# A decoder trunk on one core: moving the first weight part and the first root in the lead, and scaling the last rows on two engines

## The chip, the cores and the metric

The kernel runs on one core of a Trainium2 chip. The metric is the device time of one execution in microseconds (us). The engines work side by side, each with its own queue of instructions: PE (TensorE, matrix products and transposes), DVE (VectorE), ACT (ScalarE), POOL (GpSimd), and SP (SyncE), which here only issues transfers. Transfers are carried out by the core's 16 DMA engines; SP, ACT and POOL issue them. An instruction waits in its engine's queue until what it reads is ready, and everything behind it in that queue waits too.

## What is computed

The reference is the trunk of a decoder with two layers on 512 tokens of 1024 values. What matters here is its beginning and its end:

```
def rms_norm(x, g):
    xf = x.astype(jnp.float32)
    y = xf * lax.rsqrt(jnp.mean(xf * xf, axis=-1, keepdims=True) + EPS)
    return (y * g.astype(jnp.float32)).astype(x.dtype)
...
    b_gate, c_gate, u = jnp.split(h @ w_in, 3, axis=-1)
...
        h = rms_norm(x, norm_mix[layer])
...
        x = x + squared_relu_mlp(rms_norm(x, norm_mlp[layer]), mlp_w1[layer], mlp_w2[layer])
...
    return rms_norm(x, final_norm)
```

The split into three parts is the first product, of layer A. Between it and the final norm lie a gated short convolution with an MLP (layer A), shared keys and values, sparse attention and a second MLP (layer B). All values are float32.

## The kernel before, in words

**Form of the data.** The residual stream `X` lies transposed in on-chip memory: 8 chunks of 128 features, each with the 512 tokens along the free axis. float32 products are made of three float16 products: each operand is split into a high and a low half (`hi`, `lo`), and `mm3` (L355 to L358) multiplies hi by hi, hi by lo and lo by hi. ACT makes the high half, DVE the low one. Weights come in pieces of up to 128 x 1024 values: `load_piece` (L150) issues the transfer on SP's queue, `convert_piece` (L175) splits the piece (L202 on ACT, L203 on DVE) and then issues the next load into the place that has become free, `next_piece` (L213) hands a piece out, `ahead` (L222) converts in advance. `convert_piece` is a generator: it yields after each part that is split.

**The order of the work.** The program is traced in the order in which the Python code runs. From that a scheduler at build time makes the order of each engine's queue: among the instructions that are ready by its own reckoning the one traced first goes first, and gaps are filled with later ones. `with tc.issue_after(i):` adds a bond for the instructions traced in the block that run on the engine of `i`: they stand behind `i` in that engine's queue. It is a bond of order only; nobody waits for `i` to finish. Instructions of other engines in the same block are not bound.

**The lead** (L240 to L441, and L463). Seven products of zeros (`keep_busy`, L246) run on PE until data arrive. The norm vectors are transposed (L287) and copied by ACT (L288). `x_chunk(c)` (L386) transposes chunk c of x on PE (L389) and splits it with the norm weight (`split_gain`: L303 on ACT makes `x0h`, L304 on DVE makes `x0l`), and DVE copies it to `X` (L394). Behind the transposes of chunk 0 stand five more products of zeros. The first block p = 0 computes 256 columns each of the three parts C, u and B of the first product (accumulators `pc`, `pu`, `pb`, two banks each) chunk by chunk. Pieces 0 to 7 hold for chunk c the three parts' columns, (3, 256) values; piece 0 is loaded and split in three parts, in the order 1, 2, 0. In each turn c of the loop (L420) the products of chunk c are traced and then chunk c + 2. Piece 0 is bound behind the split of chunk 0, chunk 1 behind the first accumulator pair's products. The norm's root isn't needed for the products themselves, since the norm is applied to their results: `x_rstd` (L397) squares and sums the rows of x on ACT (L401, four tiles of 128 tokens), `rstd_of` (L309) makes 1/sqrt from it (square root on ACT at L313, the rest in small steps on DVE, L315 to L320: a reciprocal and one Newton step). `broadcast_rows` (L323) spreads it by four transposes on PE (L327), ACT copies it (L332), DVE squares it (L440), and the results of `pc`, `pu` and `pb` are multiplied by it (L470, L477, L486). In the kernel before, squares and root stand in one function, bound behind the split of chunk 5.

**The end** (L1187 to L1312). The last MLP's second product works by blocks of 256 features p = 0 to 3, with seven products for each (a scheme that saves an eighth product; `PRODUCTS`, L142) into seven half banks, and DVE adds them to `X` in `combine`. Finished blocks are brought to token order by PE's transposes (`turn_tokens`, L1207), squared with a running sum on ACT (`square`, L1202), copied to the output rows `xt` and multiplied by the norm weights `gains(p)` on POOL (`token_major`, L1211). `xt[0]` to `xt[3]` are the four tiles of 128 tokens; tiles 0 and 1 lie in the tile `xsh`, 2 and 3 in `xsl`.

For the last block (p = 3, features 768 to 1023, that is chunks 6 and 7 of `X`) `last_b` (L1238) orders the work by hand. `product(i)` is one of the seven products for the last four pieces (12 matmuls, L576). `X1` is chunk 7 and `X2` chunk 6; `n2` are tokens 0 to 255 and `n1` tokens 256 to 511. Tokens 0 to 255 are complete after product 5, chunk 7 of the others after product 1, chunk 6 of the others after product 6 and the add `final` (L1280). So the tiles 0 and 1 are transposed, squared and get their root first (`root(0)`), tiles 2 and 3 get `root(1)` at the very end. After a root the rows are finished: features 768 to 1023 are multiplied by root and norm weight in one operation on DVE (L1288, L1306, L1307), the others by the root alone (L1293, L1309 on DVE; L1296, L1304 on ACT). `put` (L1235) issues the store: whole rows of tiles 0 and 1 on SP's queue, half rows of tiles 2 and 3 on ACT's and SP's queues.

## Time and profile before

| what | value |
|---|---|
| three runs, median | 1116.23 us (1115.17 to 1118.41) |
| profiled execution | 1115.42 us |
| its span on the core | 1113.6 us |
| mean granted clock of PE | 0.998 |
| span before PE's first real product | about 7 us |
| from the last product of the last MLP to the end of the span | about 9.5 us |

The runs are timed without the profiler; the profiled execution is one more, and its span is what the trace shows of it. The rows below come from three views of that execution. In the page, engines are given with their share of the span. In a table of stretches (`a:b`) each engine has its busy time and its number of instructions, followed by the granted clock, the DMA engines' share and what they moved. In a timeline a row is: start, duration (both us), engine, line, operation, what it writes `<-` what it reads, shape, how many instructions are merged into the row, and in brackets how long the engine had been idle and who ended it. `PEld` is the loading of weights into PE, `SPq` and `ACTq` are the queues that issue transfers. Instructions of one engine overlap by some 0.1 us, since one begins while the other drains; the distance between two starts is what one costs the engine.

### The profile page before, as it was taken

What the parts mean: (1) busy time and instruction counts of PE and PEld (TensorE: products, weight loads), DVE (VectorE), ACT (ScalarE), POOL (GpSimd) and SP (SyncE); (2) the same over time, 40 slices, a digit from 0 to 9 for tenths busy, and PEclk for the clock granted to TensorE, in tenths of its full rate; (3) what the DMA queues carried; (4) which work ended last, traced back from release to release, by engine and by line L of the source; (5) the groups of instructions that cost most, each with busy time, mean ns of one, the idle gap of its engine ahead of it and who ended that gap; (6) DMA issues with size and microseconds to landing.
All of it is one profiled execution on the core that took longest, in us unless ns stands there. A gap on an engine that the chain in (4) does not pass through costs nothing.

```text
span 1113.6 us, 20039 instructions
## 1 busy us (share of the span) xinstructions
PE 1091.4 (98%) x7960; PEld 693.9 (62%) x7960; DVE 869.5 (78%) x1627; ACT 571.7 (51%) x922; POOL 58.5 (5%) x75
## 2 busy tenths in 40 slices
PE   9999999999999999999999999899999999999996
PEld 4444444446885448875767676675444788445895
DVE  5755466987988667969588889997998698875776
ACT  4532244545433444437578787875755433352352
POOL 1000000000000000000102021212000000000020
PEclk9999999999999999999999999999999999999999
DMA  6433335543333333303434242112653333330321
GB/s 214 132 97 95 114 95 151 152 119 108 114 115 115 99 109 99 111 18 119 122 98 132 66 128 63 39 40 64 184 158 106 98 118 108 114 95 1 96 77 76
DMA packets 149708, 115.74 MB, mean 104 GB/s; under 512 B 8700, under 2 KB 146640, under 8 KB 149616
## 3 DMA queue, kind: packets, MB, share of 16 engines
q1 hardware_dynamic: 146624, 108.88, 32.5%
q10 hardware_dynamic: 2608, 4.97, 1.5%
q8 instruction: 62, 1.02, 0.4%
q0 software_dynamic: 384, 0.63, 0.2%
q14 instruction: 30, 0.25, 0.1%
HBM read 110.22 MB, written 2.14 MB: 101 GB/s over the span
## 4 chain that ended last, share of the span: by engine, by line
PE 86%; DVE 7%; ACT 3%; issue 2%; POOL 1%; DMA 0%; DVEq 0%; ACTq 0%; SPq 0%
PE c L576 8%; PE a L576 8%; PE a L357 6%; PE a L356 6%; PE a L358 6%; PE b L576 6%; PE c L357 6%; PE c L358 6%; PE c L356 6%; PE b L358 6%; PE b L357 5%; PE b L356 5%; PE d L576 4%; PE e L576 2%; PE c L1007 2%
## 5 line engine op out<-in xcount | busy, mean ns | idle before, releaser
L202 ACT ACTIVATE whi<-wst 128x1024 f16<-128x1024 f32 (+3 forms) x172 | 144.3, 854 | 185.3 <-PE b L357 65.5
L203 DVE SCALAR_TENSOR_TENSOR wlo<-wst,whi 128x1024 f16<-128x1024 f32 (+3 forms) x172 | 170.1, 998 | 42.0 <-ACT whi L202 41.5
L576 PEld LDWEIGHTS <-whi 128*128 128x128 f16 x1792 | 175.3, 98 | 20.7
L358 PEld LDWEIGHTS <-wlo 128*128 128x128 f16 x1024 | 100.2, 98 | 111.7 <-DVE wlo L203 0.5
L356 PEld LDWEIGHTS <-whi 128*128 128x128 f16 x1024 | 100.3, 98 | 109.5 <-issue 2.5
L357 PEld LDWEIGHTS <-whi 128*128 128x128 f16 x1024 | 100.2, 98 | 108.4 <-issue 2.8
L189 ACT ACTIVATE whi<-wst 128x1792 f16<-128x1792 f32 x64 | 108.5, 1700 | 109.7 <-DVE wst L187 41.5
L190 DVE SCALAR_TENSOR_TENSOR wlo<-wst,whi 128x1792 f16<-128x1792 f32 x64 | 129.3, 2023 | 15.8 <-ACT whi L189 15.8
L187 DVE TENSOR_TENSOR wst<-wst 128x256 f32<-128x256 f32 x256 | 96.1, 428 | 19.6 <-DMA wst<-mlp_w_dram 18.3
L527 DVE TENSOR_TENSOR rl<-ml_z,rh 128x1792 f16<-128x1792 f32 x32 | 64.8, 2026 | 44.7 <-ACT rh L526 44.7
L576 PEld LDWEIGHTS <-wlo 128*128 128x128 f16 x896 | 87.7, 98 | 10.7 <-issue 0.2
L526 ACT ACTIVATE rh<-ml_z 128x1792 f16<-128x1792 f32 x32 | 54.3, 1696 | 57.3 <-DVE ml_z L525 57.3
L1001 ACT ACTIVATE at_p<-at_s,at_m 128x384 f32<-128x384 f32 (+3 forms) x128 | 70.8, 554 | 21.4 <-DVE at_m L999 20.5
L357 PE MATMUL b<-xsl,whi 128*128 128x512 f16 x208 | 78.9, 379 | 0.0
L358 PE MATMUL b<-xsh,wlo 128*128 128x512 f16 x208 | 78.9, 379 | 0.0
L356 PE MATMUL b<-xsh,whi 128*128 128x512 f16 x208 | 78.8, 379 | 0.0
L357 PE MATMUL c<-xsl,whi 128*128 128x512 f16 x192 | 72.8, 379 | 0.0
L356 PE MATMUL c<-xsh,whi 128*128 128x512 f16 x192 | 72.8, 379 | 0.0
L358 PE MATMUL c<-xsh,wlo 128*128 128x512 f16 x192 | 72.8, 379 | 0.0
L576 PE MATMUL c<-rh,whi 128*128 128x256 f16 x256 | 69.8, 273 | 0.0
L576 PE MATMUL c<-rl,whi 128*128 128x256 f16 x256 | 69.8, 273 | 0.0
L576 PE MATMUL c<-rh,wlo 128*128 128x256 f16 x256 | 69.8, 273 | 0.0
(318 smaller groups left out, 2549.9 us busy)
## 6 DMA issues: line engine op xcount, KB each, us to landing
wst<-mlp_w_dram SPq DMA_DIRECT2D x256, 256.0 KB, 3.4
wst<-a_w_in_dram SPq DMA_DIRECT2D x18, 512.0 KB, 3.6
wst<-w_kv_dram SPq DMA_DIRECT2D x12, 512.0 KB, 3.6
T<-ext_d ACTq DMA_DIRECT2D x4, 1056.0 KB, 6.1
wst<-a_w_out_dram SPq DMA_DIRECT2D x8, 512.0 KB, 3.5
wst<-b_w_qg_dram SPq DMA_DIRECT2D x8, 512.0 KB, 3.8
wst<-b_w_o_dram SPq DMA_DIRECT2D x8, 512.0 KB, 3.4
wst<-a_w_in_dram SPq DMA_DIRECT2D x7, 384.0 KB, 4.9
```

The source lines that it names most:

```text
L187: DVE.tensor_tensor(b[:, :, o], b[:, :, x], b[:, :, y], op=e)
L189: ACT.activation(hi, b[:, :, 1:], AF.Copy, scale=sc)
L190: DVE.scalar_tensor_tensor(lo, b[:, :, 1:], sc, hi, op0=OP.mult, op1=OP.subtract)
L202: ACT.activation(hi[:, s:e], w, AF.Copy, scale=sc)
L203: DVE.scalar_tensor_tensor(lo[:, s:e], w, sc, hi[:, s:e], op0=OP.mult, op1=OP.subtract)
L356: PE.matmul(ps, w[0], xs[0], start=start, stop=False)
L357: PE.matmul(ps, w[0], xs[1], start=False, stop=False)
L358: return PE.matmul(ps, w[1], xs[0], start=False, stop=stop)
L526: ACT.activation(rh[0][:, p], z[:, 1:8], AF.Copy)
L527: DVE.tensor_tensor(rh[1][:, p], z[:, 1:8], rh[0][:, p], op=OP.subtract)
L576: PE.matmul(acc7[i], wl if n == 1 else wh, xl if n == 2 else xh, stop=c == 7 and n == 2, start=c == 0 and n == 0 and not other, skip_group ...
L1001: ACT.activation(self.p[:, w], lg[:, w], AF.Exp, bias=mn[:, j:j + 1], scale=-1.0, accum_out=l[:, br * 4 + h:br * 4 + h + 1])
```

## The change

In the lead, the first part of piece 0 is converted ahead of chunk 0's split (bound behind the copy of the norm vectors), the other two parts behind it. `x_rstd` becomes `x_squares`, which stays behind chunk 5's split, and the root is bound behind the split of chunk 7.

At the end, product 1 is cut in two: three of its four pieces first, then the transposes of tiles 0 and 1, then the fourth piece. The last 256 features are multiplied by the norm weights on DVE, for tiles 0 and 1 ahead of the root, for tiles 2 and 3 behind the last step of the first root; they lie in `xt` then like all others. After a root each tile is only multiplied by it, one half of the row on ACT and the other on DVE (512 features each). `final` is bound behind the last step of the first root. ACT's queue gets an order by hand: square root, a square of tile 2, half of tile 0, a square of tile 3, the last squares, half of tile 1. The diff (`root_sqrt` and `first_vec` hold the instructions of L313 and L288; the lines that set them are left out):

```diff
...
-    def x_rstd():
+    def x_squares():
         ss0 = work.tile([128, 4], F32, name="ss0")
         for t in range(4):
             junk = wk[0].tile([128, D], F32, name="junk", bufs=1)
             ACT.activation(junk, xt[t], AF.Square, accum_out=ss0[:, t:t + 1])
-        return rstd_of(ss0)
+        return ss0
 
 
     ys = new_split(wk[0], "y")
@@ -416,10 +416,14 @@
                              c == 0, c == 7)
                 return mm
 
+            cv = convert_piece()
+            with tc.issue_after(first_vec.ins):
+                next(cv)
             hi = [x_chunk(0)]
+            with tc.issue_after(hi[0].ins):
+                drain(cv)
             for c in range(6):
-                with tc.issue_after(hi[0].ins) if c == 0 else nullcontext():
-                    w = next_piece()
+                w = next_piece()
                 if c == 0:
                     load_x(6, 8)
                 if c == 3:
@@ -433,7 +437,9 @@
                     drain(ahead())
                 hi.append(x_chunk(c + 2))
             with tc.issue_after(hi[5].ins):
-                r0 = x_rstd()
+                ss0 = x_squares()
+            with tc.issue_after(hi[7].ins):
+                r0 = rstd_of(ss0)
             pr = broadcast_rows(r0)
             rby = row_tile(pr, SY / (SW * SX))
             rb2 = ftile("rb2", 1)
@@ -573,8 +579,9 @@
                 xh, xl = (u[:, c, b - 1] for u in rh)
                 other = i % 2 == 1
                 for n in terms:
-                    PE.matmul(acc7[i], wl if n == 1 else wh, xl if n == 2 else xh, stop=c == 7 and n == 2,
-                              start=c == 0 and n == 0 and not other, skip_group_check=other)
+                    mm = PE.matmul(acc7[i], wl if n == 1 else wh, xl if n == 2 else xh, stop=c == 7 and n == 2,
+                                   start=c == 0 and n == 0 and not other, skip_group_check=other)
+                return mm
 
             late = last and p == 3
             for c in range(0, 4 if late else 8, 2):
@@ -598,7 +605,7 @@
                 if mid:
                     mid(p)
                 ws = [[u[:, k] for u in w] for w in (next_piece(), next_piece()) for k in range(2)]
-                last(acc7, lambda i: [product(i, 4 + k, w) for k, w in enumerate(ws)])
+                last(acc7, lambda i, ks=range(4): [product(i, 4 + k, ws[k]) for k in ks][-1])
                 return
             drain(post)
             post = combine(p, acc7, done)
@@ -1187,8 +1194,8 @@
     with pool("hidden_b") as hp:
         wk[0] = hp
         rh = first_half(hp, xs, ss)
-        xt = [work.tile([128, 2, D], F32, name=n) for n in ("xsh", "xsl")]
-        xt = [xt[t // 2][:, t % 2] for t in range(4)]
+        xsh, xsl = (work.tile([128, 2, D], F32, name=n) for n in ("xsh", "xsl"))
+        xt = [(xsh, xsl)[t // 2][:, t % 2] for t in range(4)]
         fng = [work.tile([128, S], F32, name="rb", bufs=3) for _ in range(2)]
         for half in range(2):
             nc.gpsimd.dma_start(fng[half], bass.AP(tensor=final_norm.tensor, offset=final_norm.offset + half * S,
@@ -1261,52 +1268,61 @@
             product(5)
             stt(X1[:, n2], P3, X1[:, n2])
             DVE.tensor_tensor(X2[:, n1], X2[:, n1], wv[:, 0], op=OP.add)
-            product(1)
+            mm = product(1, range(3))
+            lo, hi = slice(0, 512), slice(512, 1024)
+            tail = [u[:, :, 768:1024] for u in (xsh, xsl)]
+            early = []
+            with tc.issue_after(mm.ins):
+                for t in range(2):
+                    ps = bank("a")
+                    turn_tokens(ps, t, (6, 7))
+                    early.append(ps)
+            product(1, (3,))
             stt(X1[:, n1], P2, X1[:, n1])
-            lo, hi = slice(0, 512), slice(512, 1024)
-            early = []
             for t in range(2):
-                ps = bank("a")
-                turn_tokens(ps, t, (6, 7))
-                square(ps[:, 0:256], t, 3)
-                early.append(ps[:, 0:256])
+                square(early[t][:, 0:256], t, 3)
+                DVE.tensor_tensor(tail[0][:, t], early[t][:, 0:256], gains(3), op=OP.mult)
             r = root(0)
+
+            def scale(eng, t, at, c):
+                if eng is ACT:
+                    return ACT.activation(xt[t][:, at], xt[t][:, at], AF.Copy, scale=c)
+                return DVE.tensor_scalar(xt[t][:, at], xt[t][:, at], c, None, op0=OP.mult)
+
+            with tc.issue_after(root_sqrt[0].ins):
+                first_scaled = scale(ACT, 0, hi, r[:, 0:1])
             for t in range(2, 4):
                 ps = bank("b")
                 turn_tokens(ps, t, (7,))
-                square(ps[:, 0:128], t, 3)
-                early.append(ps[:, 0:128])
+                with tc.issue_after((root_sqrt[0] if t == 2 else first_scaled).ins):
+                    square(ps[:, 0:128], t, 3)
+                with tc.issue_after(root_op[0].ins):
+                    DVE.tensor_tensor(tail[1][:, t - 2, 128:256], ps[:, 0:128], gains(3)[:, 128:256], op=OP.mult)
             product(6)
-            final = DVE.scalar_tensor_tensor(X2[:, n1], P4, sc, X2[:, n1], op0=OP.mult, op1=OP.add)
+            with tc.issue_after(root_op[0].ins):
+                final = DVE.scalar_tensor_tensor(X2[:, n1], P4, sc, X2[:, n1], op0=OP.mult, op1=OP.add)
+            with tc.issue_after(final.ins):
+                scale(DVE, 0, lo, r[:, 0:1])
+                put(0, nc.sync)
             pc = bank("c")
             for t in range(2):
                 turn_tokens(pc[:, t * 128:(t + 1) * 128], 2 + t, (6,))
-            late = [pc[:, t * 128:(t + 1) * 128] for t in range(2)]
-            sq = ACT.activation(late_sq[:, :, 0:128], pc[:, 0:256].rearrange("p (t n) -> p t n", t=2), AF.Square)
-
-            def scale_half(t):
-                return DVE.scalar_tensor_tensor(xt[t][:, 768:1024], early[t], r[:, t:t + 1], gains(3),
-                                                op0=OP.mult, op1=OP.mult)
-
+            late = pc[:, 0:256].rearrange("p (t n) -> p t n", t=2)
+            with tc.issue_after(first_scaled.ins):
+                sq = ACT.activation(late_sq[:, :, 0:128], late, AF.Square)
             with tc.issue_after(final.ins):
-                scale_half(0)
-                DVE.tensor_scalar(xt[0][:, 0:768], xt[0][:, 0:768], r[:, 0:1], None, op0=OP.mult)
-                put(0, nc.sync)
+                DVE.tensor_tensor(tail[1][:, :, 0:128], late, gains(3)[:, None, 0:128].to_broadcast([128, 2, 128]),
+                                  op=OP.mult)
+                scale(DVE, 1, lo, r[:, 1:2])
             with tc.issue_after(sq.ins):
-                ACT.activation(xt[1][:, 0:768], xt[1][:, 0:768], AF.Copy, scale=r[:, 1:2])
-            r1 = root(1)
-            with tc.issue_after(root_half[0].ins):
-                scale_half(1)
+                scale(ACT, 1, hi, r[:, 1:2])
             put(1, nc.sync)
-            r = r1
+            r = root(1)
             for i in range(2):
                 t, c = 2 + i, r[:, i:i + 1]
-                ACT.activation(xt[t][:, lo], xt[t][:, lo], AF.Copy, scale=c)
+                scale(ACT, t, lo, c)
                 put(t, nc.scalar, lo)
-                DVE.scalar_tensor_tensor(xt[t][:, 768:896], late[i], c, gains(3, 1), op0=OP.mult, op1=OP.mult)
-                DVE.scalar_tensor_tensor(xt[t][:, 896:1024], early[t], c, gains(3)[:, 128:256],
-                                         op0=OP.mult, op1=OP.mult)
-                DVE.tensor_scalar(xt[t][:, 512:768], xt[t][:, 512:768], c, None, op0=OP.mult)
+                scale(DVE, t, hi, c)
                 put(t, nc.sync, hi)
 
         mlp_down(rh, done_b, mid_b, last_b)
```

8 lines of the change are left out of this document (4 added, 4 removed).

## The prediction, made before the changed kernel had run

> **What bounds the kernel now.** I read the page first, then busy time in stretches, then the timeline engine by engine at both ends, since the change touches only the first 40 us and the last 12.
>
> ```profile
> span 1113.6 us, 20039 instructions
> PE 86%; DVE 7%; ACT 3%; issue 2%; POOL 1%; DMA 0%; DVEq 0%; ACTq 0%; SPq 0%
> ```
>
> The chain that ended last runs through TensorE (PE) for 86% of the span. The stretches say how a gain at one end travels (columns: stretch, its length, busy time of PE, weight loads, DVE, ACT, POOL, clock, DMA share, GB/s):
>
> ```profile
> 45.10:110.00 64.90, 64.90 (x302) 29.39 (x302) 37.92 (x55) 20.04 (x25) 0.00 (x0) 1.00 0.35 107
> 560.00:860.00 300.00, 289.70 (x2710) 185.46 (x2708) 267.47 (x677) 212.37 (x499) 39.98 (x47) 1.00 0.33 97
> 860.00:1092.70 232.70, 232.70 (x1710) 167.34 (x1708) 180.61 (x276) 96.59 (x94) 5.74 (x8) 1.00 0.29 87
> ```
>
> From 45 us on PE is busy all the time except in the attention stage, 560 to 860, where 300.00 - 289.70 = 10.3 us are waits for other engines. Those engines work on what PE gave them earlier, so a lead that is shorter should move them too. I therefore count time won in the lead in full at the end. A matmul of 512 columns hands over after 64.90/302 = 0.215 us.
>
> **The lead: the root behind x's last chunk.** ACT, then PE, then DVE, around chunk 7:
>
> ```profile
> 32.56 1.04 ACT L202 ACTIVATE whi<-wst 128x1024 f16<-128x1024 f32 x1
> 33.62 1.28 ACT L313 ACT_TABLE_LOAD   x1
> 34.92 0.30 ACT L313 ACTIVATE rs_r<-ss,eps 128x4 f32<-128x4 f32 x1
> 35.12 1.04 ACT L202 ACTIVATE whi<-wst 128x1024 f16<-128x1024 f32 x1
> 36.07 0.67 ACT L303 ACTIVATE x0h<-e,vec 128x512 f16<-128x512 f32 x1
> ```
> ```profile
> 33.50 0.60 PE L389 MATMUL e<-ident,xt 128*128 128x128 f32 x4
> 35.02 0.38 PE L358 MATMUL b<-x0h,wlo 128*128 128x512 f16 x1
> 36.78 0.38 PE L356 MATMUL a<-x0h,whi 128*128 128x512 f16 x1 [1.39 <-ACT x0h L303]
> 37.65 0.38 PE L358 MATMUL b<-x0h,wlo 128*128 128x512 f16 x1
> 38.13 0.38 PE L357 MATMUL a<-x0l,whi 128*128 128x512 f16 x1
> 39.09 0.62 PE L327 MATMUL e<-ident,rs_r 128*128 128x128 f32 x4
> ```
> ```profile
> 36.19 1.23 DVE L203 SCALAR_TENSOR_TENSOR wlo<-wst,whi 128x1024 f16<-128x1024 f32 x1 [0.57 <-ACT whi L202]
> 37.34 0.75 DVE L304 SCALAR_TENSOR_TENSOR x0l<-e,vec,x0h 128x512 f16<-128x512 f32 x1
> 38.78 0.16 DVE L320 SCALAR_TENSOR_TENSOR rs_r<-rs_t,rs_r 128x4 f32<-128x4 f32 x1
> ```
>
> Chunk 7 is transposed by 33.50 + 0.60 = 34.10, but ACT is held by the table load, the root and a weight conversion until 36.07. PE waits 1.39 for x0h, and once more for x0l, which stands on DVE behind a conversion: 38.13 - 37.65 - 0.215 = 0.26. Together 1.65 us.
>
> With the root behind chunk 7's split, load and root (1.28 + 0.30) leave ACT at this place. If the conversion still goes first it takes 33.60 to 34.55 (36.07 - 35.12 = 0.95 from start to start) and x0h 34.55 to 35.22. PE wants it at 35.02 + 0.215 = 35.24: nothing, or 0.1 for the signal, is left of 1.39. On DVE the conversion moves forward with it by 1.52, to about 34.7, and x0l by as much, to about 35.85 to 36.6; PE comes to its first x0l product of chunk 7 after five matmuls, at 35.3 + 5 x 0.215 = 36.4. About 0.2 of the 0.26 stays.
>
> What is late next is the root itself. Load and root now follow x0h: 35.22 + 1.28 + 0.30 = 36.8. DVE has x0l and the copy of chunk 7 until about 37.2, then four small steps of the root, some 0.2 each: r0 at 38.0 against 38.94 now. The four transposes that spread it stand in PE's queue at 39.09 now, 1.35 earlier if they keep their place: 37.75. PE would wait 0.25 there, or nothing if the new order puts them further back; I take 0.15. If DVE puts one more conversion (1.23) between, r0 is at 39.2 and the wait 1.5. If ACT puts a conversion of 0.95 ahead of the root too, it is 2.4 and the lead loses.
>
> So: 1.65 - 0.1 - 0.2 - 0.15 = **1.2 us** won, with ends at 1.65 (no wait left) and 1.65 - 0.3 - 2.4 = -1.05.
>
> [...]
>
> **The lead: the first weight part.** Times of the load's issue, its landing (last column, us after issue), the filler matmuls and the first split:
>
> ```profile
> 1.24 1.44 SPq L165 DMA_DIRECT2D wst<-a_w_in_dram  x3
> wst<-a_w_in_dram SPq DMA_DIRECT2D x1, 128.0 KB, 2.9
> 5.51 1.75 PE L246 MATMUL c<-idle 128*128 128x512 f16 x5
> 5.82 0.69 ACT L303 ACTIVATE x0h<-d,vec 128x512 f16<-128x512 f32 x1 [0.93 <-PE d L389]
> 6.41 1.02 ACT L202 ACTIVATE whi<-wst 128x256 f16<-128x256 f32 x3
> 12.67 0.10 PEld L358 LDWEIGHTS <-wlo 128*128 128x128 f16 x1 [0.49 <-DVE wlo L203]
> ```
>
> The first part lands at 1.24 + 2.9 = 4.1, and ACT is idle for 0.93 before x0h, that is from 4.89. A conversion of 1.02/3 = 0.34 fits into that gap and delays x0h by nothing; DVE's half fits as well. But PE has its five filler matmuls until 5.51 + 1.75 = 7.26, and x0h is done at 6.51: the first product starts at 7.26 either way. What the step can win is that the six products of the first accumulator pair no longer wait their turn behind others, so chunk 1 is transposed some 0.65 (three matmuls) sooner and the conversion of the second piece ends sooner. PE's one short wait, before 12.67, of at most 0.39 - 0.215 = 0.17, should go: **+0.15**, between 0 and 0.17. If the part landed late instead, x0h would slip by up to 0.34, hidden by the 0.75 between 6.51 and 7.26. SP's queue issues the same transfers in the same order; its fourth weight load waits for the same conversions as before.
>
> **The tail.** PE, DVE and SP's queue:
>
> ```profile
> 1100.40 0.27 PE L576 MATMUL c<-rh,whi 128*128 128x256 f16 x1
> 1101.71 0.60 PE L1209 MATMUL a<-ident,X 128*128 128x128 f32 x4
> 1104.26 0.42 DVE L1280 SCALAR_TENSOR_TENSOR X<-e,X 128x256 f32<-128x256 f32 x1
> 1104.59 0.15 DVE L320 SCALAR_TENSOR_TENSOR rs_r<-rs_t,rs_r 128x2 f32<-128x2 f32 x1
> 1105.18 0.61 DVE L1293 TENSOR_SCALAR xsh<-xsh,rs_r 128x768 f32<-128x768 f32 x1
> 1105.70 0.42 DVE L1232 TENSOR_REDUCE sst<-late_sq 128x2 f32<-128x264 f32 x1
> 1105.82 1.33 SPq L1236 DMA_DIRECT2D out_dram<-xsh  x2
> ```
> ```profile
> 1107.41 1.33 ACT L1304 ACTIVATE xsl<-xsl,rs_r 128x512 f32<-128x512 f32 x2 [0.82 <-DVE rs_r L320]
> 1107.75 0.34 DVE L1307 SCALAR_TENSOR_TENSOR xsl<-b,rs_r,rb 128x128 f32<-128x128 f32 x1
> 1108.01 0.35 DVE L1309 TENSOR_SCALAR xsl<-xsl,rs_r 128x256 f32<-128x256 f32 x1
> 1108.38 1.11 SPq L1236 DMA_DIRECT2D out_dram<-xsl  x2
> ```
> ```profile
> 1106.50:1107.00 0.50, 0.00 (x0) 0.00 (x0) 0.45 (x3) 0.10 (x1) 0.00 (x0) 1.00 0.68 270
> 1107.00:1108.00 1.00, 0.00 (x0) 0.00 (x0) 0.84 (x4) 0.59 (x1) 0.00 (x0) 1.00 1.05 418
> 1111.00:1112.00 1.00, 0.00 (x0) 0.00 (x0) 0.00 (x0) 0.00 (x0) 0.00 (x0) 0.50 0.99 371
> 1112.00:1112.60 0.60, 0.00 (x0) 0.00 (x0) 0.00 (x0) 0.00 (x0) 0.00 (x0) 0.50 0.12 41
> ```
>
> The last fence decides. The output is 512 x 1024 x 4 bytes = 2.10 MB, and from about 1106.65 to 1112.1 the DMA engines are full (shares 1.05 and 0.99): 2.10 MB in 5.45 us, 385 GB/s. Nothing computed after 1109.2 ends the span; the stream of stores does, and it began 0.8 after the first store was issued at 1105.82. So **the tail is worth what the first store comes earlier**, as long as the stream doesn't run dry. [...]
>
> The new path to the first store. Three of product 1's twelve matmuls, each (1101.71 - 1100.40)/12 = 0.109, go behind the transposes of tokens 0 to 255, so these, their squares and the first root come 0.33 earlier. The root's last step stands at 1104.59 now with X's last add in front of it; without that 0.2 earlier, 1104.39, and with the 0.33 at 1104.06. The two multiplications of 256 columns by the norm weights (0.4 each, by the 0.42 of the add) have DVE's idle time before the root as cover; if they get in front of chunk 7's add or the reduction, the root loses up to 0.4. That add itself comes four transposes (0.44) later, with its own transposes; PE has product 6 to go on with, so I count nothing, at worst 0.2 of a wait. Behind the root's last step come two multiplications of 128 columns (0.26 each, 1108.01 - 1107.75) which were traced before X's last add and are ready: I take it that they go first, so the add starts at 1104.15 + 0.52 = 1104.67, which is 0.4 later than now; if the add goes first, 1104.2. Then half a row of token tile 0 on DVE: 512 columns, between the 0.26 of 256 and the 0.52 of 768 (1105.70 - 1105.18), 0.4 to the next start and about 0.48 to its end, beside ACT's half (1.33/2 = 0.67, from about 1104.3, done by 1105.0). First store: 1104.67 + 0.36 + 0.48 + 0.03 = 1105.54, against 1105.82: **0.3 us** won; 0.75 with the add first; -0.2 if the root loses its 0.4 and more.
>
> Does the stream stay full? The first two stores are 1.05 MB, 2.7 us: from 1106.35 to 1109.05. The second root follows X's last add by the same steps (reduction 1.44 after the add) plus some 0.1 for DVE's two extra operations, minus 0.1 since ACT has 512 columns instead of 768 in front of the square root. It ends 0.4 later than now, so rows 256 to 511 start at 1107.8; DVE's half is done at 1108.35 (now its three operations a tile cost 0.78, then 0.4), ACT's at 1108.5, plus 0.8 to the data: 1109.15. The stream just holds, and its backlog covers the 0.4 lost on the second root; were that root 0.4 later still, the stream would be dry for 0.4 or so and the 0.3 won would be gone. The second pair of halves is issued by 1109.2, long before 1111.8, where the stream then ends. ACT's first half row and the square of 128 columns behind it (0.3) end at 1105.3, before the last squares, which take the 0.4 ahead of the reduction at 1104.67 + 1.44.
>
> **Sum** against the profiled execution, 1115.42 us (its span and 1.8 around it): 1.2 + 0.15 + 0.3 = 1.65 us, so 1113.8. The median of the three runs, 1116.23, is 0.8 above that execution, inside their scatter of 1115.17 to 1118.41; from the median 1114.6.
>
> **Rivals.** A difference of 0.3%, 3.35 us, is about what a measurement of this kernel can tell from no change.
> 1. *The wait moves to the spreading of the first root* (PE's transposes of rs_r). For it: load and root now start when chunk 7 is split, and two conversions compete with them. Against it: nine matmuls of chunk 7 and pu's and pb's of both chunks need no root. The lead wins 0.1 instead of 1.35, the sum is 0.4: 1115.8. Chance 0.22. [...]
> 2. *Everything comes out*: add first, no wait left in the lead: 1.65 + 0.15 + 0.75 = 2.55, 1113.7. For it: if ACT takes x0h ahead of the conversion, at 34.15, both halves of chunk 7 are ready before PE asks for them. Chance 0.15.
> 3. *The tail gives back*: DVE's new multiplications stand in front of chunk 7's add and the reduction, the first root comes later and the first store 0.2 after 1105.82. 1.35 - 0.2 = 1.15, 1115.1. Chance 0.12.
> 4. *Slower, by the order of the attention stage.* The order in all queues is worked out anew for the whole program, and small differences in the lead can reorder what meets there. Its place: 560 to 860, where 10.3 us of PE waits hang on who comes first on DVE and ACT. A quarter more is 2.6, a half more 5.2: with the 1.65 won, 1117.2 to 1119.8, in the middle 1118.5. It decides from 1.65 us of added waits. Against it: nothing in that stage is edited, and a shift that is the same for all engines changes no order. Chance 0.11.
>
> **Chances and range.** My forecast has the remaining 0.40. Its own range is 1113.7 to 1115.6. Cases 1 to 3 lie within 1113.7 to 1115.8; with a scatter of about 1.2 for a median of few runs and the lower half of case 4, the range is 1112.5 to 1117.5. Faster by over 0.3% (below 1112.9) takes case 2 and luck: 0.07. Slower by over 0.3% (above 1119.6) takes the far half of case 4: 0.06. The rest, 0.87, lies within.
>
> **What would show it.** Right: the table load behind x0h of chunk 7, no wait of 1.39 on ACT's x0h, p = 1 starting about 1.3 earlier, the DMA share rising at 0.3 earlier (counted from the end of PE's products) and no gap in the stream. Wrong: a wait of PE on rs_r at the spreading of the root; a first store more than the 1.56 us of now (1105.82 - 1104.26) behind X's last add (case 3); PE waits in the attention stage clearly over 10.3 us (case 4); a DMA share below 0.9 between the second and the third store.

## The result and the profile after

The changed kernel takes 1114.85 us (median of 19 executions, 1113.48 to 1116.21); the kernel before, on the same chips and in turn with it, 1116.32 us (19 executions, 1114.67 to 1118.41). The ratio is 0.9985, with a 95% interval of 0.9979 to 0.9991: 1.5 us faster, which is within 0.3%. Forecast were 1114.6 us and 1.65 us. The profiled execution took 1114.40 us. So the time came out as forecast, but not by the terms of the forecast: the lead won more than was worked out, and the tail won nothing.

The span of that execution on the core is 1112.5 us (1113.6 before), and the chain of work that ended last has the same shares as before, PE 86%.

**The lead.** The timeline of the kernel after: PE at its first real product, around chunk 7 of x and at the start of p = 1, then ACT and DVE around chunk 7.

```profile
7.44 0.38 PE L356 MATMUL a<-x0h,whi 128*128 128x512 f16 x1
33.67 0.60 PE L389 MATMUL e<-ident,xt 128*128 128x128 f32 x4
...
35.18 0.38 PE L358 MATMUL b<-x0h,wlo 128*128 128x512 f16 x1
35.40 0.38 PE L356 MATMUL a<-x0h,whi 128*128 128x512 f16 x1
...
36.26 0.38 PE L358 MATMUL b<-x0h,wlo 128*128 128x512 f16 x1
36.88 0.38 PE L357 MATMUL a<-x0l,whi 128*128 128x512 f16 x1 [0.24 <-DVE x0l L304]
...
38.24 0.62 PE L327 MATMUL e<-ident,rs_r 128*128 128x128 f32 x4
...
42.89 1.03 PE L453 MATMUL e<-onehot,relb 32*16 32x512 f32 x2
...
32.73 1.99 ACT L202 ACTIVATE whi<-wst 128x1024 f16<-128x1024 f32 x2
34.62 0.67 ACT L303 ACTIVATE x0h<-e,vec 128x512 f16<-128x512 f32 x1
35.31 1.28 ACT L313 ACT_TABLE_LOAD   x1
36.60 0.30 ACT L313 ACTIVATE rs_r<-ss,eps 128x4 f32<-128x4 f32 x1
...
37.93 0.16 DVE L320 SCALAR_TENSOR_TENSOR rs_r<-rs_t,rs_r 128x4 f32<-128x4 f32 x1
```

Two rows of the kernel before for the comparison, its first real product and the start of p = 1:

```profile
7.10 0.38 PE L356 MATMUL a<-x0h,whi 128*128 128x512 f16 x1
...
44.17 1.03 PE L447 MATMUL e<-onehot,relb 32*16 32x512 f32 x2
```

The table load now stands behind x0h of chunk 7. x0h starts 34.62 - 33.67 = 0.95 behind the transposes, where it was 36.07 - 33.50 = 2.57, and PE's wait for it is gone: the first product that reads it (35.40) starts 0.22 behind the one ahead of it. The wait for x0l is not: 36.88 - 36.26 - 0.215 = 0.41, where it was 0.27 counted in the same way. (The 0.24 in the bracket counts only from the end of the product ahead as the profile models it.) The root's last step ends at 38.09, 0.15 before the transposes that spread it; the new order has put them behind two products of the accumulators that follow `pc`, and nobody waits. From chunk 7's transposes to the start of p = 1 it is 42.89 - 33.67 = 9.22 us, before 44.17 - 33.50 = 10.67: 1.45 won. From the first real product to chunk 7 it is 26.23, before 26.40: 0.17 won. Together 1.62, of which 1.28 stand in absolute time (42.89 against 44.17), since in this execution the first real product was 0.34 late. That is not the change, as the last section shows.

**The middle.** The stretch of the attention stage in the kernel after:

```profile
560.00:860.00 300.00, 289.69 (x2700) 185.13 (x2699) 268.12 (x677) 212.53 (x499) 40.04 (x47) 1.00 0.33 97
```

PE waits 300.00 - 289.69 = 10.31 us, as before. Between the two ends PE's products stand in the same order as before; of the other engines' work one weight conversion on DVE has another place, at the start of p = 1 (44.24 before, 49.51 after). From the start of p = 1 to the last product of the last MLP it is 1102.51 - 42.89 = 1059.62 us; before it was 1103.75 - 44.17 = 1059.58. What the lead won arrives at the tail in full.

**The tail.** The timeline of the kernel after: PE's last product, DVE, ACT, the first two stores in one row, and the last store (a narrow window, so that it stands alone).

```profile
1102.51 0.27 PE L582 MATMUL e<-rl,whi 128*128 128x256 f16 x1
...
1101.77 0.41 DVE L1284 TENSOR_TENSOR xsh<-a,rb 128x256 f32<-128x256 f32 x1
1102.10 0.15 DVE L1239 TENSOR_REDUCE sst<-ssf 128x2 f32<-128x8 f32 x1
...
1103.20 0.16 DVE L320 SCALAR_TENSOR_TENSOR rs_r<-rs_t,rs_r 128x2 f32<-128x2 f32 x1
...
1103.48 0.41 DVE L1303 SCALAR_TENSOR_TENSOR X<-e,X 128x256 f32<-128x256 f32 x1
...
1104.85 0.42 DVE L1314 TENSOR_TENSOR xsl<-c,rb 128x256 f32<-128x256 f32 x1
1105.19 0.42 DVE L1239 TENSOR_REDUCE sst<-late_sq 128x2 f32<-128x264 f32 x1
...
1106.56 0.16 DVE L320 SCALAR_TENSOR_TENSOR rs_r<-rs_t,rs_r 128x2 f32<-128x2 f32 x1
...
1104.43 0.39 ACT L1312 ACTIVATE late_sq<-c 128x256 f32<-128x256 f32 x1
...
1104.37 1.44 SPq L1243 DMA_DIRECT2D out_dram<-xsh  x2
...
1108.12 0.36 ACTq L1243 DMA_DIRECT2D out_dram<-xsl  x1
```

The same points of the kernel before that were not shown yet:

```profile
1103.75 0.27 PE L576 MATMUL e<-rl,whi 128*128 128x256 f16 x1
...
1107.22 0.16 DVE L320 SCALAR_TENSOR_TENSOR rs_r<-rs_t,rs_r 128x2 f32<-128x2 f32 x1
...
1109.16 0.33 SPq L1236 DMA_DIRECT2D out_dram<-xsl  x1
```

All runs differ by up to 3 us before they reach the tail, so the tail is counted from the start of PE's last product (1102.51 after, 1103.75 before). Counted so, in us:

| kernel | 1st root's last step | X's last add | last squares | last reduction | 2nd root's last step | 1st store | 3rd store | last store | end of span |
|---|---|---|---|---|---|---|---|---|---|
| before | 0.84 | 0.51 | 1.45 | 1.95 | 3.47 | 2.07 | 4.41 | 5.41 | 9.85 |
| after | 0.69 | 0.97 | 1.92 | 2.68 | 4.05 | 1.86 | 4.83 | 5.61 | 9.99 |
| e4 | 1.11 | 0.31 | 2.24 | 2.99 | 4.36 | 2.11 | 5.14 | 5.92 | 10.29 |
| e6 | 0.70 | 0.98 | 1.92 | 2.34 | 3.80 | 1.86 | 4.58 | 5.36 | 9.82 |
| e5 | 0.76 | 0.84 | 1.78 | 2.20 | 3.65 | 1.76 | 4.44 | 5.21 | 9.67 |
| e7 (before without the first two stores) | 0.84 | 0.51 | 1.45 | 1.95 | 3.47 | none | 4.42 | 5.41 | 9.81 |
| e8 (after without the first two stores) | 0.70 | 0.98 | 1.92 | 2.68 | 4.05 | none | 4.84 | 5.61 | 10.20 |

The first store comes 0.21 sooner, and the end 0.14 later. The page gives a span to 0.1 us only, but the other profiles agree: the end is at 9.85 to 9.92 in the four that have the old tail with all its stores (before, `e1`, `e3`, `e11`) and at 9.99 to 10.06 in the three that have the new one (after, `e2`, `e9`). The stretches of the kernel after show the gap between the second and the third store (the last two columns are the DMA engines' share and GB/s):

```profile
1106.00:1107.00 1.00, 0.00 (x0) 0.00 (x0) 0.79 (x5) 0.24 (x1) 0.00 (x0) 0.66 1.01 401
1107.00:1108.00 1.00, 0.00 (x0) 0.00 (x0) 0.71 (x2) 1.00 (x2) 0.00 (x0) 0.50 0.81 324
1108.00:1109.00 1.00, 0.00 (x0) 0.00 (x0) 0.00 (x0) 0.09 (x1) 0.00 (x0) 0.50 0.83 305
```

A share of 0.81 and 0.83 where it had to stay near 1: the stream of stores runs dry for 0.19 + 0.17, some 0.4 us.

### The profile page after: what moved, and what is told of

Same layout as the page of the kernel before. It is cut to its first block, busy times and chain, and to the rows that moved or that the text cites. A ratio compares the mean times of both kernels' runs of the same rounds, so it can differ in the third digit from the quotient of the medians.

```text
span 1112.5 us, 20040 instructions
## 1 busy us (share of the span) xinstructions
PE 1091.4 (98%) x7960; PEld 694.1 (62%) x7960; DVE 869.6 (78%) x1627; ACT 572.4 (51%) x923; POOL 58.6 (5%) x75
## 3 DMA queue, kind: packets, MB, share of 16 engines
q8 instruction: 62, 1.02, 0.4%
## 4 chain that ended last, share of the span: by engine, by line
PE 86%; DVE 7%; ACT 3%; issue 2%; POOL 1%; DMA 0%; DVEq 0%; ACTq 0%; SPq 0%
PE a L582 8%; PE c L582 8%; PE a L357 6%; PE a L356 6%; PE a L358 6%; PE b L582 6%; PE c L356 6%; PE c L358 6%; PE c L357 6%; PE b L358 6%; PE b L357 5%; PE b L356 5%; PE d L582 4%; PE e L582 2%; PE c L1014 2%
```

## The experiments

Where a ratio is given, it comes from 11 executions of the kernel; the other times are of one execution.

### The lead alone and the tail alone

`e1_lead` is the kernel before with the lead's part of the diff (conversion of the first part, squares and root parted), `e2_tail` the kernel before with all the rest of it:

```diff
+            cv = convert_piece()
+            with tc.issue_after(first_vec.ins):
+                next(cv)
...
-                r0 = x_rstd()
+                ss0 = x_squares()
+            with tc.issue_after(hi[7].ins):
+                r0 = rstd_of(ss0)
```

> The kernel before with the change's lead alone (first weight part ahead of chunk 0's split, root behind chunk 7's split); its tail is the old one. Theory A (all that the change wins comes from the lead; the tail is worth nothing): 1.3 to 1.5 us faster than before, ratio 0.9987, and from PE's last product to the end of the span the 9.85 us of before. Rival B (as predicted, the tail wins 0.3 of it): 1.0 to 1.2 us faster in the time; the same 9.85. In the trace both expect the block p = 1 to begin 1.4 us sooner after chunk 7's transposes than before (11.6 us there).

Measured: 1114.83 us, ratio 0.9988 [0.9979, 0.9996]. From chunk 7's transposes to p = 1 it is 9.23 us, from the first real product to chunk 7 26.22: the lead of the kernel after. (The 11.6 us of the expectation count to the product behind the one that is taken here for the start of p = 1: 45.13 - 33.50 in the kernel before.)

> The kernel before with the change's tail alone. Theory A: no gain, between 0.2 faster and 0.2 slower; from the last product of PE to the end of the span 9.9 to 10.0 us against 9.85 before, with a gap in the stream of stores between the second and the third store of some 0.5 us. Rival B: 0.3 faster, 9.55 us, no gap.

Measured: 1116.17 us, ratio 0.9999 [0.9991, 1.0008]. The two distances are 10.67 and 26.42, as before; the tail ends 10.06 after PE's last product, where the kernel before has 9.85, and the DMA share falls to 0.62 between the second and the third store. The interval of the time would hold a gain of 0.3 too; the place of the end does not. All of the gain is the lead's.

### What the wait in the lead was

`e3_table` is the kernel before with another operation in the warming instruction at the very start, which only loads a table. The square root's table is then loaded there, and every queue keeps its order, without the load ahead of the first root:

```diff
-    ACT.activation(warm, ones, AF.Square)
+    ACT.activation(warm, ones, AF.Sqrt)
```

> The kernel before, where only the first warming activation on ACT is a square root of ones in place of a square: its result is not used, every queue keeps its order, and the one instruction that goes is the table load in front of the first root. Theory A (the lead's wait is the table load that sat in front of chunk 7's split, and nothing of the order): x0h of chunk 7 starts at about 34.8 in place of 36.07, PE's wait of 1.39 for it shrinks to 0.1 or less, and the whole is 1.2 to 1.3 us faster, as much as the change's lead. [...] Rival D (the root's place in the order is what holds chunk 7, its table doesn't matter): no gain over 0.3.

Measured: 1114.85 us, ratio 0.9995 [0.9986, 1.0004], too little for a verdict on the time. The trace decides; PE at chunk 7's transposes, then ACT:

```profile
33.46 0.60 PE L389 MATMUL e<-ident,xt 128*128 128x128 f32 x4
...
34.60 0.67 ACT L303 ACTIVATE x0h<-e,vec 128x512 f16<-128x512 f32 x1
```

x0h starts 1.14 behind the transposes in place of 2.57. That is 1.43 less with nothing but the load taken away, and near its 1.28. Nothing else stands around the load in the kernel before: ACT goes from the conversion to the load in 0.02 (32.56 + 1.04 to 33.62) and from the load to the root in 0.02 (33.62 + 1.28 to 34.92). From chunk 7 to p = 1 it is 9.57, so taking the load away wins 1.10 where the change wins 1.45. Most of the other 0.35 are PE's waits: 0.14 for x0h (none after the change), since a conversion and the root still stand ahead of it, and 0.59 for x0l (0.41 after the change).

### What the conversions in the lead are worth

After the change ACT still converts two weight pieces (1.99 us) ahead of chunk 7's split. `e9_conv_behind` binds them behind it:

```diff
-            drain(ahead())
+            with nullcontext() if p else tc.issue_after(hi[7].ins):
+                drain(ahead())
```

> The kernel after, with the conversions of the weight pieces that stood ahead of chunk 7's split bound behind it. Theory (what is left of the wait in the lead is work of ACT and DVE that stands ahead of chunk 7's two halves): the high half of chunk 7 starts at once when chunk 7 is transposed, 0.5 us after the start of its transposes in place of 0.95, the low half follows it at once, the wait of 0.24 us on it is gone, and the first product of p = 1 comes 9.0 us after chunk 7's transposes in place of 9.22. Rival: the conversions that are pushed back are late themselves, and PE waits at the start of p = 1 for a weight piece; then that product comes at 9.2 or later. The time, 0.2 us, is below what one run can tell.

Measured: 1115.85 us in one execution, and p = 1 at 10.34 behind chunk 7, not at 9.0. ACT's x0h, one of the root's steps on DVE (L318) between two conversions (the steps L319 and L320 follow them), and PE at the spreading of the root:

```profile
34.20 0.69 ACT L303 ACTIVATE x0h<-e,vec 128x512 f16<-128x512 f32 x1 [1.48 <-PE e L389]
...
37.48 1.23 DVE L203 SCALAR_TENSOR_TENSOR wlo<-wst,whi 128x1024 f16<-128x1024 f32 x1 [0.77 <-ACT whi L202]
38.62 0.16 DVE L318 TENSOR_TENSOR rs_t<-rs_r 128x4 f32<-128x4 f32 x1
38.70 1.22 DVE L203 SCALAR_TENSOR_TENSOR wlo<-wst,whi 128x1024 f16<-128x1024 f32 x1
...
40.33 0.62 PE L327 MATMUL e<-ident,rs_r 128*128 128x128 f32 x4 [1.42 <-DVE rs_r L320]
```

The theory fell, and its rival holds by its number (9.2 or later) but not by its cause: PE waits for the root, not for a weight piece. Chunk 7's split does come at once, and x0l is not waited for any more. But DVE's halves of the pushed-back conversions come between the root's small steps, where they came back to back in the kernel after, and PE waits 1.42 for the root. This is the rival of the prediction that the kernel after escaped. The wait is about as long as was priced there, 1.5 (from start to start 40.33 - 38.54 - 0.215 = 1.58), but by other terms: two conversions came between the root's steps and not one, and the spreading stood 1.0 later in PE's queue than the prediction had it. The wait that the root causes does not vanish when its cause is moved, it is only hidden as long as nothing else is put into the same place.

### What holds the tail

The first theory was X's last add, which comes 0.46 later than before. `e4_add_first` takes it from behind the first root and puts the two multiplications of 128 columns behind it:

```diff
-                with tc.issue_after(root_op[0].ins):
-                    DVE.tensor_tensor(tail[1][:, t - 2, 128:256], ps[:, 0:128], gains(3)[:, 128:256], op=OP.mult)
+                early.append(ps)
...
-            with tc.issue_after(root_op[0].ins):
+            if True:
                 final = DVE.scalar_tensor_tensor(X2[:, n1], P4, sc, X2[:, n1], op0=OP.mult, op1=OP.add)
...
+                for t in range(2, 4):
+                    DVE.tensor_tensor(tail[1][:, t - 2, 128:256], early[t][:, 0:128], gains(3)[:, 128:256], op=OP.mult)
```

> The changed kernel, but X's last add isn't bound behind the first root, and the two multiplications of 128 columns by the norm weights stand behind it in DVE's queue. Theory A (the tail lost what it won because that add comes 0.45 later after the last product than before, so the second root is late and the stream of stores runs dry): the add 0.4 to 0.5 sooner after the last product, the gap in the stream 0.1 or gone, the end of the span 0.4 to 0.5 nearer to the last product than in the changed kernel (9.99 us), and 0.4 faster than the changed kernel: ratio to before 0.9981. Rival E (only the first store's time counts, since the stream is bound by the rate at which it is written): the first store comes at most 0.2 sooner and so does the end.

Measured: 1115.12 us, ratio 0.9992 [0.9983, 1.0001]. The timeline, PE's last product and the add:

```profile
1102.81 0.27 PE L582 MATMUL e<-rl,whi 128*128 128x256 f16 x1
...
1103.12 0.42 DVE L1301 SCALAR_TENSOR_TENSOR X<-e,X 128x256 f32<-128x256 f32 x1
```

The add comes at 0.31, but in the middle of the first root's steps, and one of the two multiplications with it; the last step comes at 1.11 in place of 0.69. ACT's order, written by hand, then holds the second root: half of tile 0 waits for the first root, a square waits behind it and the last squares behind that. They come at 2.24 (1.92 in the kernel after), and the end 0.30 later. The theory fell, but the run does not test the add by itself, since it made the first root late. It shows that the second root hangs on what stands behind the first one too.

`e6_late_mult` puts only the last multiplication (256 columns, 1104.85 in the kernel after) from ahead of the reduction to behind the second root's first step. `e5_second_root` does this too, frees the two squares on ACT from half of tile 0, and puts one multiplication of 128 columns into a gap between the first root's steps and the other behind tile 0's scaling:

```diff
+            with tc.issue_after(root_half[0].ins):
+                DVE.tensor_tensor(tail[1][:, :, 0:128], late, gains(3)[:, None, 0:128].to_broadcast([128, 2, 128]),
+                                  op=OP.mult)
...
-                with tc.issue_after((root_sqrt[0] if t == 2 else first_scaled).ins):
+                with tc.issue_after(root_sqrt[0].ins):
                     square(ps[:, 0:128], t, 3)
```

> The changed kernel, only the last multiplication by the norm weights (256 columns) behind the second root's reduction on DVE. Theory F: the reduction 0.3 sooner (2.36 after the last product in place of 2.68), the second root's last step at 3.75, the gap in the stream down from 0.5 to 0.2, the end at 9.7. Rival H (ACT's order is what holds the second root, not DVE's): the reduction not more than 0.1 sooner and the end at 9.9 or later.

> The changed kernel with the second root freed of three things that stand in front of it: both squares of 128 columns ahead of ACT's half of tile 0, X's last add straight behind the first root's last step (one small multiplication ahead of that step, one behind DVE's half of tile 0), and the last multiplication of 256 columns behind the second root's reduction. Theory F (the changed tail won a first store 0.2 sooner and lost it again because the second root comes 0.58 later after PE's last product, 4.05 against 3.47, and the stream of stores runs dry for it): second root's last step at about 3.65, first store at 1.7 (1.86), third at about 4.45 (4.83), no gap in the stream, the end at about 9.55 after the last product (9.99); in the time 0.4 faster than the changed kernel, ratio to before 0.9983. Rival G (the gap in the stream isn't what costs; the end follows the last store issued): the last store about 0.4 sooner too, so the same end, but with the gap still there.

Measured: `e6` ends at 9.82, with the reduction at 2.34 in place of 2.68 (one execution, 1116.43 us; the last experiment names what made it so long); `e5` at 9.67, time 1114.91 us, ratio 0.9984 [0.9975, 0.9993]. In `e5`, PE's last product, the second root's last step and the last store:

```profile
1103.83 0.27 PE L582 MATMUL e<-rl,whi 128*128 128x256 f16 x1
...
1107.48 0.16 DVE L320 SCALAR_TENSOR_TENSOR rs_r<-rs_t,rs_r 128x2 f32<-128x2 f32 x1
...
1109.04 0.36 ACTq L1243 DMA_DIRECT2D out_dram<-xsl  x1
```

That is 0.32 better than the kernel after and 0.18 better than before, 0.1 less than expected; `e10`, which has the same tail, ends at 9.66. The reduction 0.34 sooner rules out the rival of `e6`. The gap in the stream nearly closes, as the theory of `e5` had it and its rival did not: the lowest share between the second and the third store is 0.88 in `e6` and 0.92 in `e5`. In the time `e5` can't be told from the kernel after (0.9985); the place of the end is what shows the gain. In the table above the end follows the last store's issue by 4.37 to 4.59 in all seven kernels. From the first store it is 7.78 to 8.18, and the kernel after and `e6`, which have the same first store, end 0.17 apart.

### Whether the first stores matter

`e7_no_first_stores_before` and `e8_no_first_stores_after` leave out the stores of tiles 0 and 1, so half of the output is not written; all else is done.

```diff
-                put(0, nc.sync)
...
-            put(1, nc.sync)
```

> The kernel before without the stores of tiles 0 and 1 (their half of the output isn't written; all the arithmetic stays). Theory F (in the kernel before the stream of stores is full from the first store on and sets the end): the stores of tiles 2 and 3 meet an empty stream, the end comes about 0.4 sooner, 9.45 after PE's last product against 9.85. Rival G (the last store's own time sets the end): 9.85 as before.

> The changed kernel without the stores of tiles 0 and 1 (their half of the output isn't written; all the arithmetic stays). Theory F (there the stream is dry before the third store, so the end hangs on the second root alone and the first stores don't matter): the end within 0.15 of the changed kernel's 9.99 after the last product. Rival E (the rate of the whole stream sets it): 0.4 or more sooner.

Measured: the ends are 9.81 (before: 9.85) and 10.20 (after: 9.99), times 1117.43 and 1115.35 us, one execution each. The last store of the kernel before, in the DMA issues (KB each, then us from issue to landing):

```profile
out_dram<-xsl SPq DMA_DIRECT2D x1, 256.0 KB, 3.4
```

The same of `e7`, and its stretches:

```profile
out_dram<-xsl SPq DMA_DIRECT2D x1, 256.0 KB, 3.2
```

```profile
1111.00:1112.00 1.00, 0.00 (x0) 0.00 (x0) 0.07 (x1) 0.00 (x0) 0.00 (x0) 0.50 1.00 369
1112.00:1113.00 1.00, 0.00 (x0) 0.00 (x0) 0.00 (x0) 0.00 (x0) 0.00 (x0) 0.50 1.02 385
1113.00:1114.00 1.00, 0.00 (x0) 0.00 (x0) 0.00 (x0) 0.00 (x0) 0.00 (x0) 0.50 0.78 283
```

With 1.05 of the 2.10 MB gone the last store lands only 0.2 sooner, and after the change it lands no sooner (3.4 us behind its issue, 3.3 with all stores). So `e7` is as its rival had it. `e8` ends 0.21 later, outside the 0.15 that its theory allowed and further from its rival; why it is later stays open. The four stores of tiles 2 and 3 alone fill the DMA engines for 2.8 us (1.00 + 1.02 + 0.78 in `e7`), and they cannot begin before the second root. The backlog of the first two stores, on which the prediction counted, was worth 0.2 at most before, and nothing after. Whether the third store with these 2.8 us or the last store with its 3.3 sets the end can't be told apart here, since both are issued by the same root.

### Where the scatter comes from, and a better version

Profiles of the same middle differ by 2 us: from p = 1 to PE's last product it is 1059.6 to 1060.1 in four of them and 1060.2 to 1061.9 in seven. In those seven the mean granted clock of the profiled execution is 0.995 or 0.996, in the four it is 0.997 or 0.998. `e5` has 0.996. Two stretches of it, parted where its clock falls:

```profile
702.29:705.70 3.41, 1.66 (x20) 0.87 (x18) 2.18 (x8) 3.26 (x8) 3.18 (x4) 1.00 0.00 0
705.70:709.12 3.42, 3.42 (x21) 2.66 (x22) 2.81 (x9) 1.83 (x6) 1.44 (x2) 0.50 0.02 5
```

PE is busy for only 1.66 of the 3.41 us ahead of the fall, and behind it the clock is 0.50 for 3.42 us. In `e6`, which has the 1061.9, it is 0.50 in all of 704 to 710 and 0.65 in the us behind that. `e10_fill` is `e5` with eight products more whose result nobody uses, `e11_fill_before` is the kernel before with the same eight:

```diff
+            for _ in range(8):
+                PE.matmul(bank("a"), KD[:, 0, 0, 0, 0:128], KD[:, 0, 0, 0, :], start=True, stop=True)
             yield from out_proj(0)
```

> The kernel of e5_second_root, with eight products of 512 columns more in the stretch at 700 to 707 us where PE is idle half of the time; their result is used by nothing, they go into a bank that is free there. Theory (part of the scatter of the runs is PE's clock, which in most profiles falls to half for some 3 to 6 us behind that stretch): no stretch with a clock of 0.5 to 0.6 near 704 to 712, 1059.6 to 1060.0 us from the first product of p = 1 to the last product in place of 1061.5, a median about 1113.4 (1.5 below that of e5_second_root), ratio 0.997. Rival: the added products stand in front of the attention's own and cost what they win, or the clock falls all the same: 1114.9 to 1116.5, ratio 0.9985 to 1.000.

> The kernel before with only the eight added products of e10_fill. Theory (the added products keep the clock from falling and win that alone, whatever the two ends of the kernel do): no stretch with a clock under 0.9 near 700 to 714, no timed execution with a mean clock of 0.996 or less (37 of 56 executions of the kernel before had it), a median about 0.8 below the kernel before, 1115.6, ratio 0.9993. Rival: the gain of e10_fill over e5_second_root (1.0) was the scatter of different calls; then mean clocks of 0.995 and 0.996 stay, and the median is 1116.3 to 1117 (the added products cost up to 0.5).

Measured: `e10` 1113.91 us (1113.21 to 1115.21), ratio 0.9976 [0.9967, 0.9985], 1059.87 us through the middle; `e11` 1115.97 us, ratio 0.9996 [0.9987, 1.0006], 1059.74 us. The stretches of `e10`:

```profile
702.00:704.00 2.00, 1.88 (x21) 1.31 (x21) 0.77 (x4) 1.93 (x5) 1.89 (x2) 1.00 0.00 0
704.00:706.00 2.00, 1.24 (x8) 0.57 (x8) 2.00 (x5) 1.60 (x6) 1.89 (x2) 1.00 0.00 0
706.00:708.00 2.00, 2.00 (x24) 1.41 (x22) 1.84 (x7) 1.57 (x6) 1.14 (x2) 1.00 0.04 8
```

In `e10` PE is busy for 5.12 of these 6.00 us, in `e11` for 5.01, and the clock is 1.00 throughout in both. The mean clocks of the timed executions say the same: none of the 22 with the eight products had 0.996 or less, against 46 of 78 of the kernel before and 6 of 11 of `e5`. (The profiles of `e10` and `e11` have 0.997.) In the kernel before the 46 took 1116.8 us in the mean, and the 17 with 0.998 took 1115.65. `e10` came out 0.5 above what was expected of it, and 1.0 below `e5`, which was timed on another chip; their two intervals overlap, so the times alone do not show that gain. For `e11` the time alone decides nothing either: its interval holds both no gain and the expected 0.8, and only 4 of the 15 executions of the kernel before that were timed beside it had a low clock. `e10` has the lowest median of this study, 2.6 us below the kernel before.

## Why the prediction was right, and where it was wrong

- *Time won in the lead counts in full at the end*: right. 1.28 won at p = 1, 1.24 at PE's last product.
- *The root behind chunk 7, 1.2 us*: right in its mechanism and too low; 1.45, the same in all profiles with the change's lead but `e9`. Counted from start to start, less 0.215 for a product, PE's waits before were 36.78 - 35.02 - 0.215 = 1.55 for x0h, 0.27 for x0l and 39.09 - 38.78 - 0.215 = 0.10 at the spreading; after they are 0, 0.41 and 0.08, about 1.43 less. The prediction took x0l's wait so, but x0h's from the bracket, 1.39, which begins only where the product ahead ends as the profile models it: 0.16 too little. It also allowed 0.1 for x0h and 0.15 at the spreading, which were not paid (the order moved the spreading back), and 0.2 for x0l, where 0.41 stays. The root ends at 38.09. Chunk 7's transposes begin 0.17 later than in the execution that the forecast was worked out on, so that is 37.92 by its clock, against 38.0. `e3` shows that 1.10 of the 1.45 come with the table load alone.
- *The load and the root, 1.28 + 0.30*: right. The square root starts at 36.60, 0.01 after the load's end (35.31 + 1.28), and takes 0.30; taking the load away in `e3` moves x0h by 1.43.
- *The first weight part, 0.15*: right; 0.17, and PE's short wait in chunk 1's products, 0.17 ahead of 12.67 in the kernel before, is the one that is gone. Where the first real product came at 6.79 us or later, it is 26.22 to 26.26 to chunk 7 in all six kernels with the step, and 26.40 and 26.41 in the two without it.
- *The tail, 0.3 won*: wrong; 0.14 lost in the profile, and the tail alone is at 0.9999 in the time. The step that failed is the one that was to decide: "the tail is worth what the first store comes earlier", and with it "its backlog covers the 0.4 lost on the second root". `e7` and `e8` show that the first stores hardly hold the later ones. The second root was 0.58 later, not 0.4: the add 0.46, and 0.27 more to the reduction, behind a multiplication that was counted as some 0.1 (0.15 came back behind the reduction, where ACT's work ahead of the square root takes 0.71 in place of 0.93). Halving the rows between two engines made the last store follow the root by 1.56 in place of 1.94, which gave 0.38 back; 0.58 - 0.38 = 0.20 is what the last store lost.
- *The first store, 0.3 sooner*: 0.21, but not by its terms. The squares of tokens 0 to 255 did come 0.36 sooner, but the named risk came true: a multiplication of 256 columns got in front of the first reduction (1101.77 against 1102.10), and counted from PE's last product that reduction comes 0.14 later than before. The root's last step is 0.15 sooner all the same, above all because X's last add no longer stands in front of it.
- *The rivals.* The wait at the spreading of the first root did not appear; `e9` shows how close it was, with a wait of about its price of 1.5, though there two conversions made it and not one. "The tail gives back" was the nearest to what happened in the tail, though by the second root and not by the first store. The rival on the other side, a new order in the attention stage, is out: PE's products stand in the same order and PE waits 10.31 us there, as before.
- *The sum*: 1.62 - 0.14 = 1.48 against 1.65 forecast and 1.47 measured between the medians. The time was hit because an error of +0.27 in the lead and one of -0.44 in the tail nearly cancel, and that is luck; so is an agreement to 0.01 between medians of executions that lie some 3 us apart.

## What to carry to other kernels

When several transfers close a kernel, ask which of them cannot begin earlier and count from there; full DMA engines at the end say nothing for the first store if the last group fills them by itself (here for 2.8 us). Work that is pulled ahead of a root to shorten what follows it must not stand in front of that root's own reduction: place it into the gaps between the root's small steps, and check each of its operations against the later root too. Where PE idles, look at the granted clock of the stretch behind it too: in `e5` 3.42 us at 0.50 stand behind 3.41 us in which PE was busy for 1.66.

## What the hardware showed that was not expected

- PE's clock halves in the middle of the kernel in some executions and not in others. The mean clocks of one kernel differ so too: the kernel before had 0.996 or less in 46 of 78 timed executions and more in the other 32. In `e5` the clock falls at 705.70, behind 3.41 us in which PE was busy for 1.66. In the profile of the kernel before PE was busy for 1.72 of 3.42 us at the same place, and the clock was 1.00 there and in the 3.43 us behind (the row below is the first of the two). What decides between them was not shown. In `e5` PE was busy for all of the 3.42 us at half clock, and behind them the clock rose to 1.00.

```profile
702.85:706.27 3.42, 1.72 (x19) 1.26 (x20) 2.18 (x9) 3.32 (x6) 3.20 (x3) 1.00 0.00 0
```

- The first real product starts between 6.17 and 7.44 us, by how fast the products of zeros ahead of it run: five of them take 1.24 us in `e4`, 1.75 in the kernel before and 2.10 in the kernel after. In the kernel after they start 0.42 to 0.43 us apart, in `e4` (1.24 - 0.38)/4 = 0.22. The clock column says nothing here, since the trace's record of the clock begins only at 6.54 us of the span in the kernel before and at 7.23 in the kernel after; what sets the pace was not shown. Coming early is not all won. In `e4`, PE, and the load of x's chunk 2 into PE:

```profile
5.09 1.24 PE L246 MATMUL c<-idle 128*128 128x512 f16 x5
6.17 0.38 PE L356 MATMUL a<-x0h,whi 128*128 128x512 f16 x1
...
10.86 0.42 PEld L389 LDWEIGHTS d<-ident,xt 128*128 128x128 f32 x4 [0.64 <-DMA xt<-x_dram]
```

  The start is 1.27 earlier than in the kernel after, and chunk 7 only 0.85: the load of chunk 2 into PE waits 0.64 for chunk 2's transfer.
- The end of the span comes 1.0 us behind the landing of the last store in the kernel before (1109.16 + 3.4 = 1112.6 of 1113.6) and 1.1 us in the kernel after (1108.12 + 3.3 = 1111.4 of 1112.5).
